# Decode self-attention: query rows spread over the partitions through DRAM, or by transposes of a broadcast copy

## The chip, the cores and the metric

The kernel runs on one core of a Trainium2 chip. A core has engines that work side by side, each through its own list of instructions in order: TensorE (PE, with its weight loads shown as PEld), VectorE (DVE), ScalarE (ACT), GpSimd (POOL) and SyncE (SP, which here only starts DMAs). They wait for one another by semaphores. The metric is the device time of one execution in microseconds, the median of several runs.

## The reference, cut to what matters

One inference step of a decoder of 2 layers, for a prompt of 256 tokens and for 8 sample sequences of 4 new tokens each, which read caches of keys and values of 1024 past tokens. Each layer has three stages: a token mixer (12 heads of 64 in three groups of dilated window attention, beside a gated unit), cross-attention to 256 memory tokens, and an MLP. Of the mixer this is what the change touches:

```python
DIL_PATTERNS = ((128, 1), (512, 4), (2048, 16))      # (window, dilation), 4 heads each
q = rope_partial(proj[..., :a].reshape(B, T, N_ATT_HEADS, HEAD_DIM), pos)
k = rope_partial(proj[..., a:2 * a].reshape(B, T, N_ATT_HEADS, HEAD_DIM), pos)
...
    idx = rows[:, None] - dist[None, :]              # dist = dilation * arange(window // dilation + 1)
    kg = jnp.take(k_all, idx, axis=1)
    s = jnp.einsum('bqhd,bqjhd->bqhj', qc, kg).astype(jnp.float32) * scale
    ...
    o = jnp.einsum('bqhj,bqjhd->bqhd', pr, vg.astype(jnp.float32)) / den[..., None]
```

In groups 1 and 2 (dilation 4 and 16) each of the 4 new tokens of a sequence looks at its own cached rows: every score is a dot product of one query with one key that no other query shares.

## The kernel before

Activations lie transposed, features over the 128 partitions and 288 tokens (256 of the prompt, 32 of the samples) along the free dimension. A projection is a series of tiles of 128 output columns; each takes 24 weight matmuls on PE: `linear` splits a weight tile into a high part `wh` (ScalarE, L343) and a low part `wl` (VectorE, L344), and `mm3` (L361 to L363) adds three products per block of the contraction. Weights come as 1 MB tiles `wraw`, two tiles of columns each, cached keys and values as 512 KB tiles `cu`; both are loaded on SP's queue, in the order in which the program asks for them (class `Stream`).

The input projection of a layer (`w_in`) has 22 such tiles, the first numbers of which make queries, keys and values in a hand-written order. As each is done, `rope` evacuates it: a shuffle and a product on VectorE (L723, L724), a product and a sum on POOL (L725, L726), into the blocks 0 to 5 of `qT` and `kT`; two blocks to a group. Beside the projection run tasks, Python generators that give out work whenever the planner (class `Tasks`) has credit: a task yields a cost and a delay in nominal nanoseconds, or the name of a flag (`q2`, `k4`, `decp`) that it waits for. These numbers and priorities set the order in which the instructions stand in the program; the Tile framework then schedules each engine's list from it and puts the semaphores in.

The tasks of the mixer are `decode_scores` (first in priority for its kind), `decode_pv`, `natural` (keys and values turned back and stored, L804 to L826), `prompt_all`, and a few of the gated unit. In `decode_scores` the scores of groups 1 and 2 go this way. `query(g)` makes a tile `qb` of 128 x 1024 with one row per partition: partition 16b + c (b the sequence, c one of 16 copies) holds the 4 queries of sequence b, 256 numbers (4 heads of 64) each. A cached tile has, in partition 16b + c, keys of the same sequence; its product with `qb` (L1059 on POOL, L1061 on VectorE; layer 0 gives six of the first group's eight to POOL, layer 1 four) and a sum over 64 numbers (L1062, `st`) are the scores. There are 8 tiles in group 1 and 4 in group 2. Then `z` and PE (L1074) collect them, a softmax runs, and `decode_pv` multiplies with the cached values (L1128).

In `query` before, two transposes (L1041) bring the 32 queries into 32 rows, ScalarE copies them out (`qn`, L1043), a DMA on ScalarE's queue stores them in a DRAM tile `qd` (L1045), and a DMA on SP's queue loads `qb` from it, each row 16 times (L1048). `qb` takes one of three buffers of the tag `kt`. `query(1)` runs before the product loop, `query(2)` after the fifth product of group 1 (`QUERY_2`). Small staging tiles, `stg`, 128 x 512, have two buffers; `natural` stores keys from them.

Of the kernel before, what the change touches and what calls it, by code (L numbers as in the profile page):

```python
# [9 lines left out]
F32 = mybir.dt.float32  # L10
# [218 lines left out]
def build(ctx, tc, I, O, worder, corder, recording):  # L229
    nc = tc.nc  # L230
    V, S, G, T = nc.vector, nc.scalar, nc.gpsimd, nc.tensor
    sb = ctx.enter_context(tc.tile_pool(name="sb", bufs=1))
    pp = ctx.enter_context(tc.tile_pool(name="pp", bufs=1, space=bass.MemoryType.PSUM))
    dp = ctx.enter_context(tc.tile_pool(name="dp", bufs=1, space=bass.MemoryType.DRAM))


    def slot(shape, dt=F32, name="slot"):
        return sb.tile(shape, dt, name=name, tag="slot", bufs=8)
# [13 lines left out]
    def stg(name="stg"):  # L252
        return sb.tile([128, 512], F32, name=name, tag="stg", bufs=2)
# [4 lines left out]
    def tr(name="tr"):  # L258
        return pp.tile([128, 512], F32, name=name, tag="tr", bufs=3)
# [143 lines left out]
    ident = const[:, C_ID:C_ID + 128]  # L403
# [53 lines left out]
    for n in range(KT):  # L457
        ps = tr()
# [272 lines left out]
    def layer(l, xH, xL, norm):  # L731
        tasks.flags.clear()
        flag = tasks.flag
        qT = slot([128, 6, TOK], name="qT")
# [227 lines left out]
        def unit_transpose(parts, both=False):  # L962
            kt = sb.tile([128, 8, 128], F32, name="kt", tag="kt", bufs=3)
            for i in range(2):
                ps = tr()
                for j in range(4):
                    T.transpose(ps[:, 128 * j:128 * j + 128], parts[4 * i + j], ident)
                if both:
                    S.copy(kt[:, 4 * i:4 * i + 4].rearrange("p a k -> p (a k)"), ps)
                elif i:  # L970
                    V.tensor_copy(kt[:, 4:8].rearrange("p a k -> p (a k)"), ps)
                else:
                    S.copy(kt[:, 0:4].rearrange("p a k -> p (a k)"), ps)
            return kt

        def decode_scores():
# [42 lines left out]
            for i in range(2):  # L1019
                cu = cs.request(("g0", l, i, 0), 1)  # L1020
                kt = unit_transpose([cu[:, 128 * j:128 * j + 128] for j in range(8)], UT_ACT)
# [11 lines left out]
            qb = {}  # L1033

            def query(g):

                for pr in range(2):
                    yield f"q{2 * g + pr}"
                ps = tr()
                for pr in range(2):  # L1040
                    T.transpose(ps[0:32, 128 * pr:128 * pr + 128], qT[:, 2 * g + pr, 256:288], ident)  # L1041
                qn = sb.tile([32, 256], F32, name="qn", tag="qn", bufs=2)
                S.copy(qn, ps[0:32, 0:256])  # L1043
                qd = dp.tile([32, 256], F32, name=f"qd{g}", tag=f"qd{g}", bufs=1)
                nc.scalar.dma_start(out=qd, in_=qn)  # L1045
                qb[g] = sb.tile([128, 1024], F32, name="qb", tag="kt", bufs=3)
                src = qd.rearrange("(b t) c -> b (t c)", t=4)[:, None, :].to_broadcast([8, 16, 1024])
                nc.sync.dma_start(out=qb[g], in_=src)  # L1048

            yield from query(1)  # L1050
            yield 200, 4000
            for g in (1, 2):
                n = 8 if g == 1 else 4
                st = sb.tile([128, 128], F32, name="st", tag="st", bufs=2)[:, 0:16 * n]
                for j in range(n):
                    cu = cs.request((f"g{g}", l, j, 0), 1)
                    lag = f"split{W.done - QK_LAG}"
                    if j in (QK_POOL1 if l else QK_POOL):
                        G.tensor_mul(cu, cu, qb[g])  # L1059
                    else:  # L1060
                        behind(V.tensor_mul(cu, cu, qb[g]), lag)  # L1061
                    behind(V.reduce_sum(st[:, 16 * j:16 * j + 16], cu.rearrange("p (c d) -> p c d", d=64),  # L1062
                                        axis=AX.X), lag)
                    yield 0, QK_LATENCY
                    if g == 1 and j == QUERY_2:
                        yield from query(2)
                z = sb.tile([128, 1024], F32, name="zs", tag="kt", bufs=3)
                V.tensor_mul(z[:, 0:128 * n].rearrange("p (j b c) -> p j b c", j=n, b=8),
                             st.rearrange("p (j c) -> p j c", j=n)[:, :, None, :].to_broadcast([128, n, 8, 16]),
                             mb[:, None, :, None].to_broadcast([128, n, 8, 16]))  # L1070
                yield 0, 1500
                for j in range(n):
                    c = 128 * (g - 1) + 16 * j
                    T.matmul(s2[:, c:c + 16], z[:, 128 * j:128 * j + 128], ek, start=True, stop=True)  # L1074
                c = 128 * g
                S.copy(sm[:, 96 + c:96 + c + 16 * n].rearrange("p (k j) -> p j k", j=n),
                       s2[:, c - 128:c - 128 + 16 * n].rearrange("p (j k) -> p j k", j=n))
                yield 80 * n, 0
# [14 lines left out]
            ps = tr()  # L1093
            for g in range(2):
                c = 224 * g
# [5 lines left out]
            for b2 in range(2):  # L1101
                r = slice(64 * b2, 64 * b2 + 64)
                src = ps[r, 256:384].rearrange("p (b q j) -> p b q j", q=4, b=8)[:, b2::2]
                V.tensor_copy(diag(z2, 4 * b2, 136, 4, 32, 4, 4)[r], src)
            ps = tr()
# [62 lines left out]
        def prompt_all():  # L1168
            for p in range(2):
# [3 lines left out]
                yield from prompt_scores(p)  # L1173

        tasks.add(decode_scores(), PRIO[0])
        tasks.add(decode_pv(), PRIO[1])
        for g in range(3):
# [329 lines left out]
```

## Time and profile before

| | us |
|---|---|
| median of 3 runs | 1073.74 (1072.79 to 1076.74) |
| the profiled execution | 1073.84 |
| its span in the trace | 1072.1 |
| busy PE / VectorE / ScalarE / POOL | 1026.8 / 763.2 / 531.0 / 189.2 |
| busy POOL on the products with qb (15 of them) | 43.5 |
| time of ScalarE waiting for PE to free a weight buffer | 234.2 |

The span is the time from the first to the last instruction of the trace; 1.7 us of the measured time lie around it. A busy share is an average over stages with different limits. What a change in one stage is worth is read from that stage's timeline, where a row in brackets names how long an engine waited and which engine, tile and line ended the wait. The granted clock of PE is told as a share of full speed (2.4 GHz).

### The profile page before, as it was taken

Reading aid. Unit: us, or ns where it says so; the run is one execution under the profiler, and the core shown is the slowest. Engines: PE = TensorE matmul, PEld = TensorE weight load, DVE = VectorE, ACT = ScalarE, POOL = GpSimd, SP = SyncE. Lnnn points to the kernel's source line nnn. Section 1 sums busy time; section 2 is a strip of 40 time slices with the busy share of each in tenths; the row PEclk is TensorE's granted clock in tenths of the full one; section 3 lists DMA queues with packets and bytes.
Section 4 is the critical chain, followed back from the end, with each engine's and each line's share of the span. In section 5 each row is a group of like instructions: output and inputs, shape, how many; then the busy total and the mean of one; then the engine's idle time right before and its main releaser. Section 6 shows DMA issues by size and latency. Waiting matters only on the chain. (4 is left out here: it accounts for less than half of the span.)

```text
span 1072.1 us, 20130 instructions
## 1 busy us (share of the span) xinstructions
PE 1026.8 (96%) x8038; PEld 958.7 (89%) x8038; DVE 763.2 (71%) x1406; ACT 531.0 (50%) x1000; POOL 189.2 (18%) x151
## 2 busy tenths in 40 slices
PE   8999999999999999999988999999999999999995
PEld 7989589988799999999977985998888999999994
DVE  6698679855489756565996876897464996565656
ACT  4427546543458535353562364565353685354431
POOL 5592013000023000000448500220000410000000
PEclk8999999999999999999999999999999999999997
DMA  9999844777944555544455898447874465545431
GB/s 290 299 260 316 243 166 154 245 267 255 325 129 143 190 169 181 158 158 161 155 162 165 241 302 235 141 161 237 285 277 157 142 177 165 185 163 191 165 117 44
DMA packets 185533, 213.68 MB, mean 199 GB/s; under 512 B 5760, under 2 KB 175136, under 8 KB 185440
## 3 DMA queue, kind: packets, MB, share of 16 engines
q1 hardware_dynamic: 177216, 205.00, 60.1%
q10 hardware_dynamic: 8224, 7.41, 2.1%
q8 instruction: 63, 1.03, 0.4%
q14 instruction: 30, 0.25, 0.1%
HBM read 203.80 MB, written 8.59 MB: 198 GB/s over the span
## 5 line engine op out<-in xcount | busy, mean ns | idle before, releaser
L343 ACT ACTIVATE wh<-wraw 128x1024 fp32r<-128x1024 f32 (+1 forms) x237 | 249.3, 1054 | 285.6 <-PE acc L362 234.2
L344 DVE TENSOR_TENSOR wl<-wraw,wh 128x1024 fp32r<-128x1024 f32 (+1 forms) x237 | 308.4, 1304 | 100.1 <-ACT wh L343 99.5
L361 PE MATMUL acc<-xH,wh 128*128 128x288 f32 x728 | 219.0, 301 | 3.2 <-DVE fy L533 3.2
L363 PE MATMUL acc<-xH,wl 128*128 128x288 f32 x728 | 217.3, 299 | 2.7 <-DVE wl L344 2.7
L362 PE MATMUL acc<-xL,wh 128*128 128x288 f32 x728 | 218.5, 301 | 1.2 <-DVE xL L640 1.2
L361 PE MATMUL acc<-hH,wh 128*128 128x288 f32 x512 | 151.1, 295 | 0.0
L362 PE MATMUL acc<-hL,wh 128*128 128x288 f32 x512 | 151.1, 295 | 0.0
L363 PE MATMUL acc<-hH,wl 128*128 128x288 f32 x512 | 150.8, 295 | 0.0
L361 PEld LDWEIGHTS acc<-xH,wh 128*128 128x128 f32 x728 | 139.5, 192 | 4.4 <-issue 2.5
L363 PEld LDWEIGHTS acc<-xH,wl 128*128 128x128 f32 x728 | 138.9, 191 | 4.0 <-DVE wl L344 3.6
L362 PEld LDWEIGHTS acc<-xL,wh 128*128 128x128 f32 x728 | 139.1, 191 | 2.3 <-DVE xL L640 1.9
L551 POOL TENSOR_TENSOR s<-s,xres 128x288 f32<-128x288 f32 x15 | 20.2, 1349 | 444.8 <-DVE s L547 444.1
L361 PEld LDWEIGHTS acc<-hH,wh 128*128 128x128 f32 x512 | 96.4, 188 | 0.0
L362 PEld LDWEIGHTS acc<-hL,wh 128*128 128x128 f32 x512 | 96.4, 188 | 0.0
L363 PEld LDWEIGHTS acc<-hH,wl 128*128 128x128 f32 x512 | 96.2, 188 | 0.0
L361 PE MATMUL acc<-fH,wh 128*128 128x290 f32 x256 | 78.3, 306 | 1.8 <-DVE fy L533 1.8
L362 PE MATMUL acc<-fL,wh 128*128 128x290 f32 x256 | 76.9, 301 | 0.2 <-DVE fL L525 0.2
L363 PE MATMUL acc<-fH,wl 128*128 128x290 f32 x256 | 75.8, 299 | 0.5 <-DVE wl L344 0.5
L361 PEld LDWEIGHTS acc<-fH,wh 128*128 128x128 f32 x256 | 48.3, 189 | 2.6 <-PE acc L363 2.2
L362 PEld LDWEIGHTS acc<-fL,wh 128*128 128x128 f32 x256 | 48.5, 190 | 1.2 <-DVE fL L525 0.6
L363 PEld LDWEIGHTS acc<-fH,wl 128*128 128x128 f32 x256 | 48.1, 189 | 1.2 <-DVE wl L344 1.0
L1059 POOL TENSOR_TENSOR cu<-cu,qb 128x1024 f32<-128x1024 f32 x15 | 43.5, 2917 | 13.1 <-DMA qb<-qd 9.6
(326 smaller groups left out, 2182.2 us busy)
## 6 DMA issues: line engine op xcount, KB each, us to landing
cu<-cache_mem_kv SPq DMA_DIRECT2D x64, 512.0 KB, 7.4
wraw<-w_up SPq DMA_DIRECT2D x32, 1024.0 KB, 5.5
wraw<-w_down SPq DMA_DIRECT2D x32, 1024.0 KB, 4.8
wraw<-w_in SPq DMA_DIRECT2D x21, 1024.0 KB, 5.7
cu<-cache_kv_w SPq DMA_DIRECT2D x42, 512.0 KB, 8.5
wraw<-w_xkv SPq DMA_DIRECT2D x16, 1024.0 KB, 6.4
wraw<-w_mix_out SPq DMA_DIRECT2D x8, 1024.0 KB, 10.1
wraw<-w_xq SPq DMA_DIRECT2D x8, 1024.0 KB, 4.9
```

The costliest lines, as they stand in the source:

```text
L343: S.activation(h[:, r], raw[:, r], AF.Copy)
L344: gates[f"split{k}"] = behind(V.tensor_sub(lo[:, r], raw[:, r], h[:, r].bitcast(F32)), "dve")
L361: m = T.matmul(ps, wh[:, k], H[:, k], start=first, stop=False)
L362: T.matmul(ps, wh[:, k], L[:, k], start=False, stop=False)
L363: T.matmul(ps, wl[:, k], H[:, k], start=False, stop=last)
L551: eng.tensor_add(self.s, self.s, xres[:, n])
L1059: G.tensor_mul(cu, cu, qb[g])
```

## The change

The function `query` makes `qb` on the chip. For each of a group's two blocks ScalarE copies the block's 32 queries into a tile `qx` of 128 x 512, token by token and sequence by sequence, each number 16 times (a broadcast in the source). PE transposes `qx` in blocks of 128 columns, eight a query, into two PSUM tiles; a block holds one token of all eight sequences, 16 columns each, and comes out as 128 partitions (16b + c) by 128 features. Two ScalarE copies of 128 x 512 bring them into `qb`. The store, the load and the DRAM pool are gone. `qx` takes the staging buffers `stg`. There are four queries in the program: one for each of groups 1 and 2 in each of 2 layers. The delays change too: 1200 between the copies and the transposes, a cost of 900 behind them, and 0, 1500 in place of 200, 4000 between the first query and the products.

```diff
-    dp = ctx.enter_context(tc.tile_pool(name="dp", bufs=1, space=bass.MemoryType.DRAM))
...
                 for pr in range(2):
                     yield f"q{2 * g + pr}"
-                ps = tr()
+                qb[g] = sb.tile([128, 1024], F32, name="qb", tag="kt", bufs=3)
+                qx = []
                 for pr in range(2):
-                    T.transpose(ps[0:32, 128 * pr:128 * pr + 128], qT[:, 2 * g + pr, 256:288], ident)
-                qn = sb.tile([32, 256], F32, name="qn", tag="qn", bufs=2)
-                S.copy(qn, ps[0:32, 0:256])
-                qd = dp.tile([32, 256], F32, name=f"qd{g}", tag=f"qd{g}", bufs=1)
-                nc.scalar.dma_start(out=qd, in_=qn)
-                qb[g] = sb.tile([128, 1024], F32, name="qb", tag="kt", bufs=3)
-                src = qd.rearrange("(b t) c -> b (t c)", t=4)[:, None, :].to_broadcast([8, 16, 1024])
-                nc.sync.dma_start(out=qb[g], in_=src)
+                    qx.append(stg("qx"))
+                    src = qT[:, 2 * g + pr, 256:288].rearrange("p (b t) -> p t b", t=4)
+                    S.copy(qx[pr].rearrange("p (t b c) -> p t b c", t=4, b=8),
+                           src[:, :, :, None].to_broadcast([128, 4, 8, 16]))
+                yield 0, 1200
+                for i in range(2):
+                    ps = tr()
+                    for j in range(4):
+                        t, pr = 2 * i + j // 2, j % 2
+                        T.transpose(ps[:, 128 * j:128 * j + 128], qx[pr][:, 128 * t:128 * t + 128], ident)
+                    S.copy(qb[g][:, 512 * i:512 * i + 512], ps)
+                yield 900, 0
 
             yield from query(1)
-            yield 200, 4000
+            yield 0, 1500
```

Line numbers of the kernel after differ by one to four from those of before: its L725 is L726 of before, its L343 is L344, its L1063 is L1059, its L1066 is L1062. The costs and delays also move other work. Three places show it.

The first is ScalarE in layer 0, around the first query; `wh` are weight splits, `kt` transposed cached keys, `zn` queries laid out for new tokens. Before:

```order
L343 ACTIVATE wh<-wraw 128x1024
L973 COPY kt<-tr 128x512 x2
L1043 COPY qn<-tr 32x256
L343 ACTIVATE wh<-wraw 128x1024 x2
L1045 DMA qd_429<-qn 32x256
L764 COPY wst<-tr 128x512
```

After:

```order
L342 ACTIVATE wh<-wraw 128x1024
L1043 COPY qx<-qT 128x512
L972 COPY kt<-tr 128x512 x2
L342 ACTIVATE wh<-wraw 128x1024 x2
L1043 COPY qx<-qT 128x512
L763 COPY wst<-tr 128x512
L996 COPY zn<-qT 64x32 x2
L342 ACTIVATE wh<-wraw 128x1024
L1051 COPY qb<-tr 128x512 x2
```

The first broadcast copy stands ahead of the key copies, the second behind the two splits that followed `qn`, and the copies into `qb` behind one more split.

The second is POOL in layer 0, where the rotary work (`ro`, and the sums into `qT` and `kT`) and the products `cu` share the engine. Before:

```order
L726 TENSOR_TENSOR kT<-ro 128x288
L1059 TENSOR_TENSOR cu<-cu,qb 128x1024 x4
L725 TENSOR_TENSOR ro<-ro,const 128x288 x2
L1059 TENSOR_TENSOR cu<-cu,qb 128x1024
L726 TENSOR_TENSOR kT<-ro 128x288
L1059 TENSOR_TENSOR cu<-cu,qb 128x1024
L726 TENSOR_TENSOR kT<-ro 128x288
L1059 TENSOR_TENSOR cu<-cu,qb 128x1024 x3
```

After:

```order
L1063 TENSOR_TENSOR cu<-cu,qb 128x1024 x2
L724 TENSOR_TENSOR ro<-ro,const 128x288
L1063 TENSOR_TENSOR cu<-cu,qb 128x1024 x2
L724 TENSOR_TENSOR ro<-ro,const 128x288
L725 TENSOR_TENSOR qT<-ro 128x288
L724 TENSOR_TENSOR ro<-ro,const 128x288
L1063 TENSOR_TENSOR cu<-cu,qb 128x1024
L725 TENSOR_TENSOR qT<-ro 128x288
L724 TENSOR_TENSOR ro<-ro,const 128x288
L1063 TENSOR_TENSOR cu<-cu,qb 128x1024
L725 TENSOR_TENSOR kT<-ro 128x288
L724 TENSOR_TENSOR ro<-ro,const 128x288
```

The six products of group 1 now stand ahead of the sums for the queries of group 2 and the third key block; before, those queries' sums came first and two keys' sums stood behind four and five products.

The third is VectorE in layer 1, where the reduce `st` of a product, the low halves `wl` and the rotary work alternate. Before:

```order
L1062 TENSOR_REDUCE st<-cu 128x16
L723 STREAM_SHUFFLE ro<-acc 128x288
L724 TENSOR_TENSOR ro<-acc,const 128x288
L1062 TENSOR_REDUCE st<-cu 128x16
L344 TENSOR_TENSOR wl<-wraw,wh 128x1024
L1061 TENSOR_TENSOR cu<-cu,qb 128x1024
```

After:

```order
L1066 TENSOR_REDUCE st<-cu 128x16
L722 STREAM_SHUFFLE ro<-acc 128x288
L723 TENSOR_TENSOR ro<-acc,const 128x288
L768 TENSOR_TENSOR wbd<-tr,const 32x128
L343 TENSOR_TENSOR wl<-wraw,wh 128x1024
L1066 TENSOR_REDUCE st<-cu 128x16
L722 STREAM_SHUFFLE ro<-acc 128x288
L723 TENSOR_TENSOR ro<-acc,const 128x288
L1066 TENSOR_REDUCE st<-cu 128x16
L343 TENSOR_TENSOR wl<-wraw,wh 128x1024
```

The low half `wl` that stood behind the second reduce of before stands one reduce earlier, and the next `wl` stands behind two more reduces.

On PE the two L1041 of layer 0's first query (behind 138 weight matmuls) become two transposes behind matmul 144 and six behind matmul 167; those of its second query move from matmul 288 to 364 and 374. In layer 1, counted from its first weight matmul, the first query's move from 168 to 217 (in one batch of eight), the second's from 321 to 383.

## Rows read from the trace of the kernel before

**Rows 1.** The page: busy us of each engine, share of the span, instructions

```profile
PE 1026.8 (96%) x8038; PEld 958.7 (89%) x8038; DVE 763.2 (71%) x1406; ACT 531.0 (50%) x1000; POOL 189.2 (18%) x151
```

**Rows 2.** Stretches: window, length, busy PE, PEld, DVE, ACT, POOL, clock, DMA share, GB/s

```profile
19.00:110.00 91.00, 88.35 (x669) 84.34 (x668) 74.52 (x130) 43.96 (x88) 52.99 (x33) 0.98 0.97 296
553.00:641.00 88.00, 80.80 (x578) 75.36 (x579) 71.04 (x139) 38.70 (x81) 48.29 (x32) 0.92 0.75 234
```

**Rows 3.** PE's timeline: start, length, instruction, [wait ahead of it <- what ended it]

```profile
38.60 0.40 PE L363 MATMUL acc<-xH,wl 128*128 128x288 f32 x1 [0.45 <-DVE wl L344]
...
74.70 0.42 PE L804 MATMUL tr<-const,kT 128*128 128x128 f32 x1 [2.20 <-POOL kT L726]
...
129.61 0.42 PE L1128 MATMUL o<-cu,z 128*32 128x256 f32 x4 [0.75 <-DMA cu<-cache_kv_w]
...
564.78 0.28 PE L1041 MATMUL tr<-const,qT 128*32 128x128 f32 x1 [1.34 <-POOL qT L726]
...
567.42 0.33 PE L804 MATMUL tr<-const,kT 128*128 128x128 f32 x1 [0.77 <-POOL kT L726]
...
586.04 0.40 PE L363 MATMUL acc<-xH,wl 128*128 128x288 f32 x1 [1.80 <-DVE wl L344]
...
589.19 0.47 PE L804 MATMUL tr<-const,kT 128*128 128x128 f32 x1 [0.77 <-POOL kT L726]
...
654.44 0.42 PE L1128 MATMUL o<-cu,zp 128*32 128x256 f32 x4 [1.52 <-DMA cu<-cache_kv_w]
```

**Rows 4.** Stretches behind two of these waits, columns as in rows 2

```profile
74.70:78.20 3.50, 3.50 (x16) 3.44 (x17) 3.50 (x8) 1.06 (x1) 3.50 (x2) 0.52 1.09 335
586.00:594.00 8.00, 7.20 (x30) 5.96 (x31) 8.00 (x10) 0.84 (x2) 8.00 (x6) 0.57 0.65 214
```

**Rows 5.** Timelines along the query's path, layer 0, last row layer 1

```profile
34.87 0.39 PE L1041 MATMUL tr<-const,qT 128*32 128x128 f32 x2
35.02 0.38 PE L361 MATMUL acc<-xH,wh 128*128 128x288 f32 x1
...
35.30 0.36 ACT L1043 COPY qn<-tr 32x256 f32<-32x256 f32 x1 [3.36 <-PE tr L1041]
...
44.87 0.71 SPq L1048 DMA_DIRECT2D qb<-qd  x1
...
54.91 1.83 DVE L1061 TENSOR_TENSOR cu<-cu,qb 128x1024 f32<-128x1024 f32 x1
...
575.72 1.22 DVE L1061 TENSOR_TENSOR cu<-cu,qb 128x1024 f32<-128x1024 f32 x1 [2.68 <-DMA qb<-qd]
```

**Rows 6.** Transposes of cached keys on PE, layer 0; last: lowest, median, highest ns

```profile
29.85 1.47 PE L967 MATMUL tr<-const,cu 128*128 128x128 f32 x12
31.07 0.38 PE L361 MATMUL acc<-xH,wh 128*128 128x288 f32 x1
...
L967 PE MATMUL tr<-const,cu x16: 272/273/273, 29.8 to 33.9; 128*128 128x128 f32 x16
```

**Rows 7.** ScalarE: copies from PSUM (ns); waits of its splits (us, count, longest)

```profile
L973 ACT COPY kt<-tr x36: 562/585/600, 30.5 to 772.5; 128x512 f32<-128x512 f32 x36
...
ACT wh L343 <- PE acc L362: 234.2, 127, 5.6
```

**Rows 8.** PE's timeline: ends of a run of 96 weight matmuls, layer 0

```profile
45.84 0.38 PE L361 MATMUL acc<-xH,wh 128*128 128x288 f32 x1
...
58.72 0.27 PE L1041 MATMUL tr<-const,qT 128*32 128x128 f32 x1
```

**Rows 9.** POOL: the products' group in ns; a rotary product and a sum in us

```profile
L1059 POOL TENSOR_TENSOR cu<-cu,qb x15: 2357/3363/3413, 55.6 to 612.3; 128x1024 f32<-128x1024 f32 x15
...
53.10 0.81 POOL L725 TENSOR_TENSOR ro<-ro,const 128x288 f32<-128x288 f32 x1 [0.65 <-DVE ro L723]
...
53.99 1.67 POOL L726 TENSOR_TENSOR kT<-ro 128x288 f32<-128x288 f32 x1
```

**Rows 10.** VectorE's timeline ahead of the wait at 586.04

```profile
582.59 1.22 DVE L1062 TENSOR_REDUCE st<-cu 128x16 f32<-128x1024 f32 x1 [0.42 <-POOL cu L1059]
583.73 2.25 DVE L344 TENSOR_TENSOR wl<-wraw,wh 128x1024 fp32r<-128x1024 f32 x1
```

## The prediction

> **What bounds the kernel now.** I read the busy shares first: TensorE (PE) is busy 1026.8 us of the span, 96%, with VectorE at 71%, ScalarE at 50% and GpSimd (POOL) at 18% [rows 1]. So the time is PE's own work plus the few places where PE stands or runs slowly, and other engines matter only where PE waits for them. The chain that ended last holds nothing but a tail on VectorE, so I went to the two stretches in which the edited function runs, the input projections of the two layers. In the table by stretch, layer 0's has PE busy 88.35 of 91.00 us at a granted clock of 0.98, layer 1's 80.80 of 88.00 at 0.92 [rows 2]. In layer 1, then, there is something to win; in layer 0 less.
>
> PE's timeline with its waits shows where. Layer 0: 0.45 us for the low half of a weight split, 2.20 for a key after rotary, and, later, 0.75 for a load of cached values. Layer 1: 1.34 in front of the query's own transposes, 0.77 for a key, 1.80 for a low half, 0.77 for a key, 1.52 for cached values [rows 3]. Behind the two largest the clock falls. From 74.70, behind 2.20 us of standing, it is 0.52 for 3.5 us, near the lower level (1.2 of 2.4 GHz), and 3.50 x 0.48 = 1.7 us are lost; around 586 to 594 it is 0.57, and 7.20 x 0.43 = 3.1 us are lost [rows 4].
>
> **What goes.** In a query, two transposes, a ScalarE copy to qn (0.36 us), a store to DRAM on ScalarE's queue and a 512 KB broadcast load on SP's. In layer 0 the transposes run at 34.87, the load is issued at 44.87, and the first multiply with qb starts at 54.91 [rows 5]. In 20 us of detour no engine is busy with it; what it costs is the late start of the multiplies, and 2 x 512 KB of DMA per layer.
>
> **What comes, PE.** 8 transposes of 128x128 per query, 16 a layer, against 4 small ones. Their price: 12 transposes of cached keys begin at 29.85 and the next weight matmul begins at 31.07, so 1.22 / 12 = 0.102 us on the queue, though one record lasts 0.272 [rows 6]. The removed ones took 0.15 for two, from 34.87 to the matmul at 35.02 [rows 5]. So 16 x 0.102 - 4 x 0.075 = +1.33 a layer, **+2.7** for both. All of it is on PE, hence on the path; it is the one certain cost. Upwards it is bounded by the record's full length (rival C), downwards by nothing free: below 0 it can't be.
>
> **What comes, ScalarE.** Four copies of 128x512 per query (two broadcasts qx, two from PSUM into qb) at about 0.585 each, 16 in both layers, less four qn: 16 x 0.585 - 4 x 0.36 = 8 us. The broadcast form, with inner steps of zero, doesn't occur in this trace; I bound it by the copies of the same output, 0.562 to 0.600, and by twice that should such reads be slow. ScalarE's weight splits wait 234.2 us in all for PE to free a buffer [rows 7], which is the cover; it is gone where ScalarE's copies stand just ahead of a split that PE needs next. Such a place is the 0.45 us at 38.60 [rows 3]: before, the qn copy stands between the splits there. By the order the first broadcast now stands earlier, ahead of the key copies, and the second behind the two splits, so I take **-0.45** away, with +0.6 (one copy in the way) as the other end.
>
> **What moves, POOL in layer 0.** PE has done 148 weight matmuls at 38.60. The query's last six transposes now stand behind matmul 167, and 19 x 0.134 us later (96 matmuls run from 45.84 to 58.72 [rows 8]) is 41.1; with 0.8 for eight transposes, less the 0.45, and 0.6 and a handoff for the last copy, qb is there at about 42.4 instead of 54.9. The multiplies start earlier, and POOL's order has six of them, with four rotary products and two query sums, ahead of the sum that makes the third key block (kT), which PE's transposes behind matmul 336 need; before, the sum that PE waited for at 74.70 had five multiplies ahead. PE comes there at 45.84 + 144 x 0.134 + 0.8 - 0.45 = 65.5. POOL: a multiply takes 2.36 us alone and 3.36 or more beside VectorE, a rotary product 0.81, a sum 1.67 [rows 9]. So the key is ready at 42.4 + 6 x 2.36 + 4 x 0.81 + 3 x 1.67 = 64.8, or with 3.36 at 70.8: a wait of 0 to 5.3, the middle 2.3. The wait of 2.20 before [rows 3] was of the same kind, so I keep it and its slow clock: **0**.
>
> **What moves, layer 1.** The old transposes stood right behind the rotary sum of the query and cost PE 1.34; the new ones stand 49 matmuls later, when the sum is long done: **-1.34**. The key wait of 0.77 at 567.42 stays [rows 3]. The stall at 586 has this cause: VectorE's reduce waits for POOL's multiply, ends at 583.81, and only then does the split of 2.25 us start for which PE stands [rows 10]. In VectorE's new order that split stands ahead of every reduce of a POOL product, but the next one has two such reduces ahead, and the multiplies begin hardly earlier: at 564.78 + 49 x 0.134 - 1.34 + 0.8 + 0.6 = 571.4 at the earliest, against 575.72 [rows 5], and POOL again has multiplies ahead of the next key. Of 1.80 + 0.77 + 3.1 = 5.7 us I take half, **-2.8**; the ends are 0 and -5.7.
>
> **What moves, DMA.** SP's queue loses the two loads that waited for the store, and cache loads behind them move forward; 1 MB less passes per layer. The waits for cached values, 0.75 and 1.52 [rows 3], are of PE on loads; I take half of each, -0.4 and -0.8, together **-1.2**, the ends 0 and -2.3. No engine waits longer for these queues: four issues fewer on each.
>
> **Sum.** +2.7 - 0.45 + 0 - 1.34 - 2.8 - 1.2 = -3.1. The profiled run took 1073.84, of which 1072.1 is the span and 1.7 lies around it; that is 0.1 over the median of 1073.74. 1073.84 - 3.1 = 1070.7.
>
> **Rivals.**
> A, the whole tangle goes. If the early qb lets all query products of both layers pass before PE's keys and splits fall due, the 2.20 and its 1.7 of clock, the 5.7 of layer 1, 0.45 and 1.34 vanish: 11.4 - 2.7 = 8.7 less, 1065.1. For it: qb comes 12 us earlier in layer 0, and POOL is idle most of the time. Against it: the multiplies only move to where rotary products are most frequent.
>
> B, POOL's early multiplies delay the keys; slower. The place is layer 0, behind matmul 336: it decides against the change from the point at which a multiply takes over 2.84 us on average, for then the wait passes 2.20. At 3.36 it is 5.3 instead of 2.20, +3.1; the next key follows 0.81 + 1.67 later with about 0.7 us of PE work between, +1.8; a second slow stretch of the clock costs 1.7; and in layer 1 the same queueing leaves the 5.7 and the loads as they are. 3.1 + 1.8 + 1.7 + 2.7 - 0.45 - 1.34 = +7.5, 1081.3. For it: the average over all multiplies is 2.92, and VectorE is busy with splits all through that stretch. Against it: some multiplies of before took 2.36 in the midst of such work [rows 9].
>
> C, transposes cost their full length and cost the clock. 32 x 0.272 - 8 x 0.075 = 8.1 instead of 2.7, +5.4; three batches of six or eight, each 2 us like the standing at 74.70, then bring 1.7 of slow clock each, +5.1: 1081.2. Against it: after 12 transposes in a row the weight matmul follows at once [rows 6] and the stretch has a clock of 0.98 [rows 2]. The Trainium skill, "TensorE: Matmul & The Clock Gate", Part 4, has a PE transpose at some 275 ns in a kernel and says that it does not count as busy for the clock; by that this rival would be the result. The trace has the same length for one record and not the same price.
>
> D, nothing is felt: PE's added work is paid, and the only gains are 0.45 and 1.34. 1073.84 + 2.7 - 1.8 = 1074.7. That is also the case in which the multiplies aren't earlier where it counts, so that the change doesn't do what it says.
>
> **How the numbers follow.** Chances: the forecast 0.50, A 0.27, B 0.14, D 0.05, C 0.04. About 0.5%, 5.4 us, is what a measurement of this kernel can tell from no change: faster is below 1068.4, slower above 1079.1. A lies below in four of five cases (0.22), the forecast's lower end adds 0.08: faster 0.30. B lies above in most (0.11), C (0.03), the forecast's upper end 0.04: slower 0.18. The rest, 0.52, is the same. For the range I leave out the lower part of A, where the load waits go too (1063 and less, 0.08), and the upper half of B and C (0.10): 1063 to 1080.
>
> **What would show each step.** The new transposes: their group should have 32 instructions in all, with the next weight matmul about 0.1 us per transpose behind the first, and no fall of the clock behind them. The query: the first multiply of layer 0 at 42 to 44. POOL: the wait of PE for a kT in layer 0, at about 66, near 2; over 5 means B, none means A. Layer 1: no wait in front of a query's transposes, and PE's wait for a low half at about 584 under 1 us; if it is still 1.8, half of the gain is gone. Loads: the waits for cached values near 0.4 and 0.8. The prediction is wrong as a whole if a new wait appears that none of these rows has, first of all a broadcast copy on ScalarE that stands behind a staging buffer's store, since qx shares its two buffers, or if the cached keys come later than the query.

## The result

The changed kernel takes 1090.99 us (median of 6 runs, 1087.42 to 1094.88) against 1073.26 of the kernel before (6 runs, 1070.69 to 1076.74). The ratio is 1.0167, with a 95% interval of 1.0135 to 1.0198: slower by 17.7 us, where 3.1 us faster was forecast. The profiled run took 1087.42, the shortest of the six, 13.6 more than the profiled run of before. What follows explains those 13.6 by the trace, and the whole by runs. An execution can fall into a second, slower state; of all those below this was so for one of e5 (1096.87), which is left out.

PE's timeline gives the stages of a layer: the projection ends with its last weight matmul, the tail ends with the first matmul of the output projection, the output projection with the first of cross-attention. Lengths in us, for the two kernels and for five runs that are told of below (k2 and p1 are one program, with the order of the old instructions held in k2 and free in p1; p3 and p6 hold it on some engines only):

| | projection 0 | tail 0 | output 0 | projection 1 | tail 1 | output 1 |
|---|---|---|---|---|---|---|
| before | 98.5 | 27.3 | 29.9 | 114.0 | 26.1 | 29.2 |
| after | 104.5 | 27.9 | 31.0 | 107.9 | 33.3 | 31.3 |
| n1 (one number changed) | 106.1 | 25.7 | 30.8 | 106.3 | 32.4 | 29.3 |
| k2 (new way, order held) | 96.4 | 27.2 | 29.8 | 111.8 | 27.6 | 29.2 |
| p1 (new way, order free) | 108.6 | 25.0 | 31.2 | 111.4 | 27.6 | 28.8 |
| p3 (PE held alone) | 106.1 | 29.9 | 29.8 | 114.6 | 25.9 | 29.1 |
| p6 (VectorE and POOL held) | 100.4 | 26.7 | 29.8 | 112.3 | 29.6 | 29.2 |

Between the layers (360 us in both kernels) and behind the second mixer (1.5 us more) there is little.

Two things limit what this table can say. The stages are cut at fixed instructions, and PE's other matmuls move across the cuts: beside the weights, projection 0 holds 178 matmuls in before and 213 in after (12 of the 35 are the transposes, net), tail 0 holds 243 and 222, projection 1 holds 194 and 198, tail 1 230 and 240. Some of the 6.1 us that projection 1 gains is work that now lies in the tail. And each row is one execution: that of p1 took 1082.75, where the median of p1 is 1090.4.

### The profile page after: what moved, and what is told of

It is laid out like the page before. It is cut to its first block, busy times and chain, and to the rows that moved or that the text cites. A ratio compares the mean times of both kernels' runs of the same rounds, so it can differ in the third digit from the quotient of the medians.

```text
span 1084.9 us, 20155 instructions
## 1 busy us (share of the span) xinstructions
PE 1030.9 (95%) x8062; PEld 960.9 (89%) x8062; DVE 772.5 (71%) x1406; ACT 539.0 (50%) x1012; POOL 187.0 (17%) x151
## 5 line engine op out<-in xcount | busy, mean ns | idle before, releaser
L343 DVE TENSOR_TENSOR wl<-wraw,wh 128x1024 fp32r<-128x1024 f32 (+1 forms) x237 | 313.6, 1326 | 105.1 <-ACT wh L342 104.5
L360 PEld LDWEIGHTS acc<-hH,wh 128*128 128x128 f32 x512 | 96.4, 188 | 0.0
L1063 POOL TENSOR_TENSOR cu<-cu,qb 128x1024 f32<-128x1024 f32 x15 | 41.9, 2813 | 19.2 <-ACT qb L1051 19.2
```

The lines of the kernel that those rows point to most:

```text
L343: gates[f"split{k}"] = behind(V.tensor_sub(lo[:, r], raw[:, r], h[:, r].bitcast(F32)), "dve")
L360: m = T.matmul(ps, wh[:, k], H[:, k], start=first, stop=False)
```

## The profile after

The page's line on busy time, as rows 1:

```profile
PE 1030.9 (95%) x8062; PEld 960.9 (89%) x8062; DVE 772.5 (71%) x1406; ACT 539.0 (50%) x1012; POOL 187.0 (17%) x151
```

PE is busy 4.1 us longer, ScalarE 8.0, as much as the copies were priced at. The span is 12.8 longer, so most of it is standing. PE's timeline with its longer waits, as rows 3:

```profile
61.93 0.40 PE L362 MATMUL acc<-xH,wl 128*128 128x288 f32 x1 [3.00 <-DVE wl L343]
...
72.44 0.30 PE L1000 MATMUL sc<-kT,zn 128*128 128x32 f32 x1 [0.47 <-POOL kT L725]
...
127.23 0.42 PE L1132 MATMUL o<-cu,zp 128*32 128x256 f32 x4 [0.45 <-DMA cu<-cache_kv_w]
...
129.18 0.42 PE L1132 MATMUL o<-cu,z 128*32 128x256 f32 x4 [0.26 <-DMA cu<-cache_kv_w]
...
131.41 0.42 PE L1132 MATMUL o<-cu,z 128*32 128x256 f32 x4 [0.53 <-DMA cu<-cache_kv_w]
...
133.99 0.56 PE L1132 MATMUL o<-cu,z 128*32 128x256 f32 x3 [1.14 <-DMA cu<-cache_kv_w]
...
146.56 0.40 PE L361 MATMUL acc<-attL,wh 128*128 128x288 f32 x1 [1.79 <-DVE attL L886]
...
658.30 0.42 PE L1132 MATMUL o<-cu,zp 128*32 128x256 f32 x4 [0.43 <-DMA cu<-cache_kv_w]
...
660.76 0.42 PE L1132 MATMUL o<-cu,z 128*32 128x256 f32 x4 [0.76 <-DMA cu<-cache_kv_w]
...
663.14 0.42 PE L1132 MATMUL o<-cu,z 128*32 128x256 f32 x4 [0.25 <-DMA cu<-cache_kv_w]
...
665.53 0.42 PE L1132 MATMUL o<-cu,z 128*32 128x256 f32 x4 [1.27 <-DMA cu<-cache_kv_w]
...
675.33 0.30 PE L1153 MATMUL tr<-const,od 128*128 128x128 f32 x1 [1.49 <-DVE od L1146]
...
676.61 0.43 PE L360 MATMUL acc<-attH,wh 128*128 128x288 f32 x1 [0.86 <-ACT attH L885]
...
678.78 0.61 PE L361 MATMUL acc<-attL,wh 128*128 128x288 f32 x1 [1.26 <-DVE attL L886]
```

The 2.20 for a key and the 1.34 and 1.80 of layer 1 are gone. In their place stand 3.00 for a weight's low half in layer 0, and in both tails four waits for cached values where there was one: 2.38 us instead of 0.75, and 2.71 instead of 1.52. Around the start of the output projections PE also stands longer for the attention's last results (`od`, `attH`, `attL`, made by VectorE and ScalarE): 1.79 at 146.56, where before has 1.02 and 0.18, and 1.49, 0.86 and 1.26 in layer 1, where before has 1.27. The clock falls too. Stretches of after, columns as in rows 2, from the end of the first projection into the output projection, and the second output projection:

```profile
110.00:158.92 48.92, 44.36 (x348) 31.38 (x349) 28.43 (x96) 20.68 (x50) 0.00 (x0) 0.93 0.69 190
676.61:707.94 31.33, 30.07 (x209) 29.72 (x210) 23.45 (x46) 15.25 (x27) 6.53 (x6) 0.89 0.30 100
```

In the kernel before, these stages have a granted clock of 1.00. By an estimate from these rows, 44.36 x 0.07 + 30.07 x 0.11 = 6.4 us are lost to it. Shorter stretches show what stood ahead of each fall:

```profile
133.00:139.00 6.00, 5.01 (x37) 2.81 (x39) 1.22 (x3) 1.80 (x7) 0.00 (x0) 0.72 1.08 253
148.00:152.00 4.00, 4.00 (x21) 4.00 (x21) 0.00 (x0) 0.00 (x0) 0.00 (x0) 0.60 0.00 0
658.00:675.00 17.00, 13.26 (x117) 7.49 (x117) 7.86 (x30) 6.14 (x20) 0.00 (x0) 1.00 1.08 309
675.00:687.00 12.00, 9.54 (x50) 8.98 (x51) 4.72 (x20) 2.31 (x4) 0.00 (x0) 0.72 0.03 10
```

The first fall stands among the waits for cached values, the second behind the wait of 1.79 for `attL`. In layer 1 the clock is 1.00 through all four waits for cached values and falls behind the waits of 1.49, 0.86 and 1.26. So only about 1.4 of the 6.4 us (5.01 x 0.28) stand beside the waits for loads.

Now the new wait of 3.00. VectorE and ScalarE ahead of it:

```profile
52.85 3.42 DVE L1065 TENSOR_TENSOR cu<-cu,qb 128x1024 f32<-128x1024 f32 x1
56.19 1.21 DVE L1066 TENSOR_REDUCE st<-cu 128x16 f32<-128x1024 f32 x1
...
58.06 1.20 DVE L1066 TENSOR_REDUCE st<-cu 128x16 f32<-128x1024 f32 x1
59.19 2.69 DVE L343 TENSOR_TENSOR wl<-wraw,wh 128x1024 fp32r<-128x1024 f32 x1
...
57.73 0.62 ACT L1043 COPY qx<-qT 128x512 f32<-128x512 f32 x1 [4.50 <-POOL qT L725]
```

VectorE's own product and two reduces stand ahead of the split that PE wants, without a gap. VectorE is also slower: the product takes 3.42 us where the first one of before took 1.83, and the splits lengthen. The low halves of both kernels from 40 to 70 us, before and then after (busy us, mean ns of one):

```profile
L344 DVE TENSOR_TENSOR wl<-wraw,wh 128x1024 fp32r<-128x1024 f32 x9 | 14.1, 1574 | 0.3
```

```profile
L343 DVE TENSOR_TENSOR wl<-wraw,wh 128x1024 fp32r<-128x1024 f32 x7 | 15.0, 2146 | 0.6 <-ACT wh L342 0.6
```

In this stretch POOL is busy 24.25 us in before and 28.00 in after. The prediction had a multiply on POOL at 2.36 or 3.36 us by what VectorE does; here VectorE's instructions are longer beside a busier POOL. On ScalarE the broadcast copy waits 4.50 us for a query sum that stands behind POOL's products, with the next high half queued behind it; PE had no wait for that half. Loads feel it too. SP's queue in after, then in before:

```profile
52.95 0.37 SPq L148 DMA_DIRECT2D wraw<-w_in  x1
57.42 5.98 SPq L148 DMA_DIRECT2D cu<-cache_kv_w  x3
...
66.74 0.38 SPq L148 DMA_DIRECT2D wraw<-w_in  x1
```

```profile
51.81 0.38 SPq L148 DMA_DIRECT2D wraw<-w_in  x1
...
60.12 0.39 SPq L148 DMA_DIRECT2D wraw<-w_in  x1
61.25 2.76 SPq L148 DMA_DIRECT2D cu<-cache_kv_w  x2
...
69.17 0.37 SPq L148 DMA_DIRECT2D wraw<-w_in  x1
```

Between 53 and 66 us after issues no weight load. The three cache loads ahead of it wait for VectorE's reduces and the `ro` step behind one, and the load itself goes out at 66.74, when the low half that frees its buffer has ended (63.67 to 66.72). In before the loads at 51.81, 60.12 and 69.17 also follow such a split, by 0.02 to 0.03 us. So it is VectorE that times them. The ten microseconds from 60 to 70 then read, in before and in after (columns as in rows 2):

```profile
60.00:70.00 10.00, 10.00 (x72) 9.12 (x71) 9.58 (x18) 3.81 (x11) 10.00 (x5) 1.00 1.00 316
```

```profile
60.00:70.00 10.00, 8.07 (x48) 7.87 (x48) 10.00 (x11) 2.08 (x4) 10.00 (x8) 0.83 0.57 181
```

VectorE has no free moment (it was busy 9.58 before), and the DMA engines move 181 GB/s instead of 316. From 20 to 120 us the averages are 263 and 287 GB/s, so over that time after has moved 2.4 MB less, of which 1 MB are the two loads of qb that it doesn't need.

## The experiments

Each time stands against runs of the kernel before on the same chip.

### Parts of the change, with the order left to the scheduler

The change has two parts, the way of the query and the planner's numbers. **e1** has the numbers alone:

```diff
+                yield 0, 1200
                 nc.sync.dma_start(out=qb[g], in_=src)
+                yield 900, 0
...
-            yield 200, 4000
+            yield 0, 1500
```

> The kernel before with its way through DRAM, and only the planner's numbers of the change: a delay of 1200 ahead of the broadcast load, a cost of 900 behind it, and 0, 1500 in place of 200, 4000 behind the first query. Theory N (the numbers do it: a cost of 900 twice a layer pushes prompt work out of the projection into the tail, where cached values are waited for): slower than before by most of the 17.9 us, 1085 to 1091. Theory P (the early qb does it: the scheduler lets the products start earlier, and they stand in the way of rotary work and loads): within 3 us of before, 1071 to 1077. Theory W (the new work itself, transposes and copies): as P, 1071 to 1077.

1079.12 against 1071.17, ratio 1.0073 (1.0045 to 1.0102): 8 us for numbers, neither theory's value. **e2** has the new way with old numbers (no `yield 900, 0`; `200, 4000` behind the first query; the 1200 between copies and transposes stays).

> The changed kernel with the old numbers as far as the program allows it: no cost of 900, and 200, 4000 behind the first query; the delay of 1200 between copies and transposes stays. N: most of the loss gone, 1074 to 1078 (before plus 2.7 of transposes). P and W: as slow as the changed kernel, 1087 to 1092.

1088.74, ratio 1.0164 (1.0121 to 1.0206): the whole loss, by the way alone. The two parts don't add up. **e3** delays the products (`yield 0, 6000`).

> The changed kernel with the products 4.5 us (nominal) later: 0, 6000 in place of 0, 1500 behind the first query. The order moves two key sums of layer 0 ahead by one product or rotary step only, so P in its narrow form (products ahead of rotary work) expects 1 to 4 us of the loss back, 1086 to 1089; N and W expect no change, 1089 to 1092.

1094.22, ratio 1.0219 (1.0181 to 1.0257): nothing comes back, against theory P's narrow form. **e5** adds the new work to the kernel before and throws it away (broadcast copies into a PSUM tile, transposes of a constant, a copy in place).

> The kernel before with the new work added and its results thrown away: per query two broadcast copies of 128x512 on ScalarE, eight transposes of 128x128 of a constant on PE, two more copies of 128x512; the way through DRAM stays, and POOL's order is that of before. W: the whole loss is there, 1087 to 1092. N and P: only 32 transposes at 0.102 us, 3.3, and little for ScalarE: 1075 to 1079.

1082.0, ratio 1.0103 (1.0066 to 1.0140): 11 us for work priced at 3.3. Its copies take two more PSUM tiles than the change does, so it isn't clean. **g3** is: transposes of a constant alone.

```diff
+                yield 0, 1200
+                for i in range(2):
+                    ps = tr()
+                    for j in range(4):
+                        T.transpose(ps[:, 128 * j:128 * j + 128], const[:, C_MQ + 128 * j:C_MQ + 128 * j + 128], ident)
...
-            yield 200, 4000
+            yield 200, 2800
```

> The kernel before with eight transposes of a constant per query added on PE, into two PSUM tiles that nobody reads; nothing on ScalarE. At 0.102 us each: 1074 to 1077. If the PSUM tiles of transposes are what is short, or the balance of the tail tips by a few us on PE: 1080 to 1088.

1090.06 against 1072.08, ratio 1.0151 (1.0106 to 1.0196). **g2** is its counterpart, the change without its transposes (`S.copy(qb[...], qx[i])`).

> The changed kernel without the eight transposes of a query: the two last copies read qx instead of PSUM (the scores are wrong). If PE's 32 transposes and their PSUM tiles make the loss: 1072 to 1079. If they cost only their 0.102 us each and the ScalarE copies and the early products make the rest: 1083 to 1090.

1086.5, ratio 1.0133 (1.0101 to 1.0165). So transposes alone cost 18 us, and the change without them 14. Prices of work can't look like this.

### Theories on the early products and on the tail

**f2** puts POOL's products behind the fourth key block's sum (an edge without a semaphore) and lets the product loop wait for the third and fourth key block (`yield "k2"`, `yield "k3"` for `yield 0, 1500`), **f3** gives the kernel before an early qb for nothing (a broadcast load of an input, no query path).

> The changed kernel with the products on POOL ordered behind the rotary sum of the fourth key block, so that POOL's order of layer 0 is nearly that of before while the query still goes by transposes. E (early products hold up rotary sums, the broadcast copies behind them and the weight splits behind those): 1074 to 1081. W (the copies and transposes): 1085 to 1091. T: in between, by what the tails then do.

> The kernel before with no spreading at all: qb is loaded by the same kind of broadcast load from an input, with no wait for the queries' store (two transposes, copy and store left out; the scores are wrong). POOL's order then mixes products and rotary sums early, as in the changed kernel. E: slower than before by 8 to 18, 1079 to 1089, although less is done. W: 1068 to 1073.

f2: 1094.17 against 1072.27, ratio 1.0226 (1.0186 to 1.0265). f3: 1075.93, ratio 1.0031 (1.0009 to 1.0053). Theory E falls on both sides: late products don't help, and early ones come with a loss of only 4. **f1** leaves the last four value tiles of a layer out, in either kernel (`cu = cs.request(...) if g < 2 else cu`).

> The kernel before, with 4 of the 14 value tiles of each layer left out: the third group's products read the last tile of the second group instead (so its output is not the reference's). Theory T (the end of each mixer hangs on the loads of the last value tiles, 2 MB less to load per layer): little to win before, whose waits there were 0.75 and 1.52: 1066 to 1073. Theory E (products too early on POOL) says nothing of it: 1069 to 1073.

> The changed kernel with the same 4 value tiles per layer left out. T: its waits for cached values (2.4 and 2.7) and the slow clock behind them go, and it comes within 6 us of the kernel before with the same tiles left out: 1072 to 1078. E or W (the loss is made in the projection or by the work itself): the distance of 12 to 18 stays, 1082 to 1090.

1072.16, ratio 1.0009 (0.9987 to 1.0032), and 1078.13, ratio 1.0064 (1.0039 to 1.0089). As theory T expected, the distance falls from 18 to 6. In the second program the first projection is as long as in after (104.3 us), and its tail is 4.3 shorter, at a clock of 1.00. So about two thirds of the loss show in the tails, through their loads; why these come late is still open. The order was free here too, but it is nearly that of after: all 151 POOL instructions and all but 9 of VectorE's 1406. The rest of the loss stays: the second output projection again begins behind waits of 1.49, 0.87 and 1.50 us and has a clock of 0.89, so that fall was not made by the loads. **g1** takes the broadcast copies from ScalarE to POOL, **h1** gives the cached tiles a sixth buffer (for one of the eight small tiles `e`).

> The changed kernel with the broadcast copies (qx) on POOL in place of ScalarE. If the loss is made by ScalarE, whose copies wait for POOL's query sums with weight splits queued behind them (8.3 us of such waits in the changed kernel): 1074 to 1082. If it is made by the loads of the tail and whatever delays them, not by ScalarE's queue: 1084 to 1094.

> The changed kernel with six buffers of cached tiles in place of five (one of the eight small tiles e given up for the room). If the value loads come too late because buffers come free late, one more of them lets half a megabyte go ahead of the tail: 1074 to 1083. If the loads are late because the DMA engines have no room, or the loss is elsewhere: 1085 to 1092.

1098.65, ratio 1.0243 (1.0213 to 1.0274), and 1092.36, ratio 1.0190 (1.0154 to 1.0225): neither remedy helps. Every program so far has another order than before in many places, far from what was changed too, and each with all value tiles loaded is slower. That is a theory of its own, and the next runs are made for it.

### The order held

The program is built twice. The first build is the kernel before, and each engine's order is read from it. The second is the kernel to be run, where edges between neighbours (no semaphores, no waits) put the old instructions into that order; only the new ones go where the scheduler likes:

```diff
+        seq = [mine[index[p]] for p in order.get(e, ()) if p not in gone]
+        for x, y in zip(seq, seq[1:]):
+            tc.add_manual_dep(y, x.name, dep, reason="held order")
```

**k1** is the kernel before plus the transposes of g3 (without their delays; the same program with the order free was not run), **k2** the new way with the old numbers, in two halves through one tile `qx` of its own, in the room of `qn`.

> The kernel before plus the same eight transposes of a constant per query on PE, but with the order of all its other instructions held on every engine as it stands in the kernel before (edges between neighbours, no semaphores); the transposes themselves go where the scheduler puts them. Theory O (the new order that the scheduler makes of any change costs the time): before plus 32 x 0.102 = 3.3, 1074 to 1077. Theory W (the transposes and their PSUM tiles cost it): as with the order left free, 1084 to 1092.

> The changed way itself (broadcast copies, transposes and copies in place of the store and the load, in two halves through one staging tile of its own) with the order of all other instructions held as in the kernel before. O: about the forecast without its moved terms, 1069 to 1076. W or E (the copies in ScalarE's queue, early products): 1083 to 1092.

k1: 1071.42 against 1072.22, ratio 0.9982 (0.9967 to 0.9997). k2: 1071.95, ratio 1.0002 (0.9987 to 1.0017). By their traces VectorE's and POOL's instructions and SP's loads stand in the order of before, all of them. With the order held the work costs nothing that can be measured. **n1** is the opposite, another order and no other work: `yield 200, 3000` for `yield 200, 4000`.

> The kernel before with one number of the planner changed and no work: 200, 3000 in place of 200, 4000 behind the first query, which moves some hundred instructions in the order. O: slower, 1076 to 1090, for nothing but another order. W or E: 1070 to 1075.

1085.03, ratio 1.0133 (1.0098 to 1.0167). **p1** is the control of k2, the same program with no order held; **p3** holds PE's alone, **p6** that of VectorE and POOL.

> The same program as the run with the new way in two halves, with no order held: every engine in the order that the scheduler makes. It is the control of that run. Theory O (the order costs it): 1080 to 1092. If it is near 1072, the gain came from the two halves and the own staging tile, not from the order.

> The same, with the order held on PE alone; loads, VectorE, POOL and ScalarE are free. If it is PE's order (what PE has to do beside the value loads in the tail) that decides: 1070 to 1077. If it is the order of products, splits and loads: 1080 to 1092.

> The same, with the order held on VectorE and POOL; the order of loads then comes out as before by itself, and PE and ScalarE are free (181 rows of PE differ). If products, splits and loads decide: 1070 to 1077. If PE's order decides: 1080 to 1092.

p1: 1090.4 against 1071.28, ratio 1.0189 (1.0143 to 1.0235). p3: 1084.83, ratio 1.0126 (1.0094 to 1.0159). p6: 1076.19, ratio 1.0055 (1.0029 to 1.0081). VectorE's and POOL's order bring back 14 of p1's 19 us, and SP's loads then come in the order of before too. PE's alone is not shown to bring anything: the median of p3 is 5.6 lower than that of p1, but the two intervals overlap. The last 5 come back in k2, where PE and ScalarE are held as well. Part of p6's 14 is seen in its first projection (100.4 us, p1 108.6), and from 60 to 70 us again, in p1, p3, p6 and k2:

```profile
60.00:70.00 10.00, 8.21 (x61) 7.72 (x62) 10.00 (x12) 6.11 (x14) 10.00 (x9) 1.00 0.56 174
```

```profile
60.00:70.00 10.00, 3.76 (x15) 2.58 (x16) 10.00 (x13) 3.62 (x8) 10.00 (x9) 0.62 0.61 192
```

```profile
60.00:70.00 10.00, 10.00 (x79) 9.60 (x78) 8.32 (x17) 5.58 (x13) 10.00 (x6) 1.00 1.01 327
```

```profile
60.00:70.00 10.00, 9.31 (x69) 8.75 (x70) 9.60 (x18) 4.71 (x12) 10.00 (x5) 1.00 1.00 331
```

With VectorE's order free, it is busy throughout and the loads run at 174 and 192 GB/s; with it held, PE is busy and they run at 327 and 331. Holding PE's order on top of VectorE's new one makes PE stand: 3.76 us busy of 10. The low halves from 40 to 70 us go the same way, in p1 and then in k2:

```profile
L399 DVE TENSOR_TENSOR wl<-wraw,wh 128x1024 fp32r<-128x1024 f32 x8 | 18.3, 2301 | 0.0
```

```profile
L397 DVE TENSOR_TENSOR wl<-wraw,wh 128x1024 fp32r<-128x1024 f32 x9 | 13.8, 1546 | 0.6 <-ACT wh L396 0.4
```

p3 has 2.04 us for one, p6 1.56. That the longer splits are what makes the loads late is a reading of these traces; no run changed them alone. It isn't the way of every loss either: n1 has 1.57 there, and 291 GB/s from 20 to 120 us, and waits 2.04 and 3.49 us for cached values in its tails. In k2 SP's weight loads are back at the times of before, with the queue otherwise free of qb:

```profile
51.85 0.37 SPq L148 DMA_DIRECT2D wraw<-w_in  x1
...
60.12 0.38 SPq L148 DMA_DIRECT2D wraw<-w_in  x1
...
69.17 0.37 SPq L148 DMA_DIRECT2D wraw<-w_in  x1
```

and the only wait for cached values in layer 0's tail is

```profile
125.67 0.42 PE L1196 MATMUL o<-cu,z 128*32 128x256 f32 x4 [0.37 <-DMA cu<-cache_kv_w]
```

No run is faster than the kernel before by what can be told apart; k1 and k2 equal it.

## Why the prediction was wrong, step by step

**What goes and what comes** was priced rightly. The transposes, broadcast copies and the first product read, in after:

```profile
40.32 0.82 PE L1050 MATMUL tr<-const,qx 128*128 128x128 f32 x6
40.89 0.38 PE L360 MATMUL acc<-xH,wh 128*128 128x288 f32 x1
...
L1050 PE MATMUL tr<-const,qx x32: 270/272/273, 35.0 to 612.2; 128*128 128x128 f32 x32
L1043 ACT COPY qx<-qT x8: 603/619/623, 26.5 to 601.5; 128x512 f32<-128x512 f32 x8
...
42.00 2.40 POOL L1063 TENSOR_TENSOR cu<-cu,qb 128x1024 f32<-128x1024 f32 x1 [3.71 <-ACT qb L1051]
```

Six transposes take 0.57 us of the queue, 0.095 each, where 0.102 was taken, and a broadcast copy 0.62, where 0.585 was. The first product starts at 42.00; qb was forecast for 42.4. By k1, 32 transposes cost nothing measurable even as a net addition, so even the 2.7 was too much. That they lie in waits that PE has anyway is likely and not shown: in k1 the wait of 2.20 is 1.36 and that of 1.34 is 0.47, but other waits grew. Rival C is out: one record is 0.272 long as feared, but the price is another, and the granted clock behind each batch in after is 1.00. The 0.45 at 38.60 is gone, as forecast.

**POOL in layer 0** (the term 0, bounds of a wait of 0 to 5.3). The queue came out as worked out: the third key block's sum ran from 65.59, so the key was ready at 67.39, by the middle of the bounds (64.8 and 70.8).

```profile
65.59 1.80 POOL L725 TENSOR_TENSOR kT<-ro 128x288 f32<-128x288 f32 x1
...
69.79 0.27 PE L803 MATMUL tr<-const,kT 128*128 128x128 f32 x1
```

But PE came at 69.79, not at 65.5, so it didn't wait there. It had already stood 3.00 for a low half, with a slow clock after it. So the term 0 failed, and not by its number alone: projection 0 became 6.0 longer, where +0.9 was forecast (1.33 - 0.45 + 0). The step looked at POOL alone. qb also frees VectorE's own products and all the reduces, and these stood ahead of a split; and it lengthened POOL's multiplies by what VectorE does, but left VectorE's own instructions at their length, where a split went from 1.57 to 2.15 us. Rival B had early products in the way of something, and put it on the wrong engine; f3, whose products are early too, loses only 4 us, so early products as such are not the price.

**Layer 1.** -1.34 and -2.8 were forecast for the projection, -4.1, or -2.8 with its transposes. It became 6.1 shorter, with the waits of 1.34 and 1.80 gone and a granted clock of 0.98 where it was 0.94. The mechanism was right and its size too small; part of the 6.1 is only moved, since eight other matmuls left for the tail.

**DMA** (the term -1.2). Here is the step that failed most. "The waits for cached values, 0.75 and 1.52: I take half of each" came from bytes, 1 MB less per layer. They rose to 2.38 and 2.71. Tails and output projections got 11.0 us longer, 9.3 of them in layer 1; the waits for loads are 2.8 of it, and the rest are the waits for `od`, `attH` and `attL`, the slow clock, and matmuls that moved there from projection 1. f1 puts about 12 us on the value loads, directly or by what comes late behind them. In the traces what decides is not how many bytes there are but when SP's queue may issue them, and that hangs on VectorE's reduces and splits, which release the buffers. The forecast saw the cache loads move forward and counted it as a gain; it had no term for the releases.

**The sum as a whole.** It priced the moved places that its rows showed and took everything else as standing still. n1 shows what that leaves out: 13 us for one number that moves instructions and adds none. k2 against p1 shows it for this change: with the order held, the new way costs 0, with the order free 19. All thirteen programs whose order the scheduler was free to change, with all value tiles loaded, lost from 4 to 27 us. The range of the forecast, 1063 to 1080, had no term for that.

What stays open: which of the moved instructions on VectorE and POOL carries most of the 14 us (no run moves one alone), why all thirteen orders lost, and whether one better than that of before exists.

## What to carry to other kernels

Where a scheduler orders the instructions from modelled times, a change costs its work and its new order, and the second can be far the larger (here 19 us, against work that cost nothing measurable); hold the old order by edges between neighbours and run the new work in it before judging either. In the forecast, follow what the released data lets start on every engine, and above all which buffer releases, and so which loads, then come later. Look at how full the stage is: from 20 to 120 us the kernel before has its DMA engines busy at 0.94 and PE at 97%. That this is why other orders lose there is an argument, not shown.

## What was not expected of the hardware

Transposes can be had for nothing: 32 more of them, 0.095 to 0.102 us each on the queue, left the time at 0.9982 of before with the order held. An instruction of VectorE has no fixed length here: the same split took 1.55 to 1.57 us on average in k2 and before and 2.30 in p1, where POOL was busy all the 30 us. And a wait can cost more than itself: behind the waits of 1.49, 0.86 and 1.26 us at layer 1's output projection the granted clock was 0.72 for 12 us, by an estimate 9.54 x 0.28 = 2.7 us more.
